# A transformer layer on one core: the loads of its first microseconds queued in another order, later tiles of x loaded into an operand's space, and matrix products of constants put on TensorE

## The chip, the core and the metric

The kernel runs on one core of one Trainium2 chip. Its engines run side by side and meet at semaphores: TensorE (PE in the profile; its weight loads are PEld), VectorE (DVE), ScalarE (ACT), GpSimd (POOL) and SyncE (SP). SP, ACT and POOL also issue DMAs, each from its own queue. SP's and ACT's are hardware queues, POOL's is a software queue.

The metric is the time of one execution on the device in microseconds. A kernel is run several times and the median is taken. Beside these runs one execution is recorded by the hardware profiler, and all rows shown come from that one.

## The reference

One encoder layer over 1024 tokens of width 1024, all in float32: half a step of a gated feed-forward net, a mixture of two kinds of attention, and another half step, each between two RMS norms. What the change touches is the beginning of the first net:

```python
def rmsnorm(x, g):
    xf = x.astype(jnp.float32)
    y = xf * lax.rsqrt(jnp.mean(xf * xf, axis=-1, keepdims=True) + NORM_EPS)
    return (y * g.astype(jnp.float32)).astype(x.dtype)

def swiglu(x, w_gate, w_up, w_down):
    return (jax.nn.silu(x @ w_gate) * (x @ w_up)) @ w_down

h = swiglu(rmsnorm(x, ffn1_pre_g[l]), ffn1_w_gate[l], ffn1_w_up[l], ffn1_w_down[l])
x = x + 0.5 * rmsnorm(h, ffn1_post_g[l])
```

The sum of squares of each token must be known, its root taken, and the token scaled by it and by the gain, before the first product with `w_gate` can be made.

## The kernel before

**Numbers.** A float32 matrix is split into a high part that TensorE takes at its quick type (`float32r`) and a low part, the rest: ScalarE copies the high part, VectorE subtracts it to get the low one. A product is then three: high by high, high by low, low by high. The big products use a seven-product scheme over 2 by 2 blocks, so operands appear as blocks with names: `A11`, `A12`, `A22` are parts of x itself, `S1` to `S4` are sums of parts. `Operand` (line 186) holds them; `self.x[b]` has two tiles, high and low, of 128 x 4 x 512.

**Tiles of x.** x is eight tiles of 128 tokens by 1024 columns. Tiles 0 to 3 are the upper half of the tokens and give `A11` (their left 512 columns) and `A12` (their right 512). Tiles 4 to 7 give the lower half, `A22` and the sums. TensorE transposes each 128 x 128 piece against an identity (`transposed`, line 169; four pieces make one group, PE L174), ScalarE copies the group out as the high part (`transpose_in`, L181), and VectorE makes the low part (L182).

**The head** is the stretch from line 1618 to 1752 in `layer`. In it the orders of PE, DVE and ACT are written out by hand (`ordered(DVE, ACT)`): each of them runs its instructions in the order of the code. After `order.close()` only PE's order stays by hand, and a scheduler places the work of the other engines. POOL's and SP's are always the scheduler's.

1. SP and ACT each load one half of x's tiles 0 and 1 (line 1643: the left halves by SP, the right ones by ACT). SP also loads the gain, one row of 1024 numbers, into the first partition of a tile `xn[0]` (line 1645). ACT loads tile 2 (line 1654), SP tile 3 (line 1655), and SP the first two weights in halves (lines 1653 and 1657) and the third whole (`w2`, line 1658).
2. `spread_gain` (line 342) lays the gain's row out over all 128 partitions by a product: a column of ones, one partition high, by the row, in two halves of 512 columns (L349). Two copies on ScalarE (L350) bring the halves from PSUM to SBUF; the code calls them `gains[0]()` and `gains[1]()` at places of its choice.
3. ScalarE loads its table for the square root (line 1698). It then squares and sums tile 0, and the left half of tile 1 (`square`, L166); VectorE does the right half of tile 1 (L1671). `rstd_by_sqrt` (line 331) adds the halves (L335, L336), takes the root on ScalarE (L337; `next(root)` stops behind it), and refines the reciprocal on VectorE (L324 to L327; the second `next(root)`).
4. `scaled` multiplies a half of a tile by its root and the gain on VectorE (L1678). `op0.one(t, keeps)` transposes a half of tile t and splits it. Copies that only save the transposed tile (`keep`, L264) are put off in the list `keeps`.
5. `hi0`, `lo0` and so on split the halves of the first three weights (L1689 on ScalarE, L1692 on VectorE). `pg.mm` makes products of one weight: for each `k` of four a high by high (L471) and a high by low (L472), then the four low by high (L477). The first products take only 256 columns (tiles 0 and 1), since tiles 2 and 3 come later.
6. `soon` is set for the third weight alone. `self.c.step()` within `mm` runs what is put off in `c.steps`, here the transposes of the right halves of tiles 2 and 3.

**Behind the head**, `pg.ahead` runs the eleven first weights through the products with `A11` and `A12`, while `F(4, 5)` and `F(6, 7)` norm the tiles 4 to 7 (squares L166, scaling L229) and `U(t)` transposes them and builds the blocks `A22` and `S1` to `S4` (`left_half`, `right_half`; casts L303, low parts L304, sums L315 to L318 and L307). The tiles 4 to 7 are loaded by POOL (line 1630) in two pairs into the buffers that tiles 0 to 3 leave. Weights in this stretch are fetched by SP (L495) when a buffer has been split.

**Places.** `Operand.second(place)` (line 197) sets aside the tiles of `S1` to `S4` and `A22` when the stage begins. They are not filled until `right_half` of tile 4. Until then, one tile of `S3` (`place`) holds the first three saved products (`op0.place[:, b]`, line 1745).

**Matmul banks.** `c.psm` has six PSUM banks under one tag, taken in turn; a bank is taken again when all its readers are done.

Of the kernel before, what the change touches and what calls it, by code (L numbers as in the profile page):

```python
# [10 lines left out]
F32 = mybir.dt.float32  # L11
F32R = mybir.dt.float32r
# [6 lines left out]
SEQ, D, DFF = 1024, 1024, 2816  # L19
P, T = 128, 512  # L20
# [8 lines left out]
A11, S2, S1, S4, A12, S3, A22 = range(7)  # L29
# [73 lines left out]
class Weights:  # L103
# [30 lines left out]
    def next(self):  # L134
        return self.ready.popleft()
# [50 lines left out]
class Operand:  # L186
# [2 lines left out]

    def __init__(self, c, gain, which):  # L190
        self.c, self.gain, self.x, self.parts, self.open = c, gain, {}, {}, 0
        self.half, self.raw, self.tied = {}, {}, False
        for b in (A11, A12):
            self.x[b] = [c.xa.tile([P, 4, T], F32R, tag=f"x{b}{i}", name=f"x{b}{i}") for i in range(2)]
        self.saved = [c.dr.tile([P, 2, T], F32, name=f"xn{which}_{t}") for t in range(4)]

    def second(self, place=False):
        tile = self.c.xb.tile
        for b in (S1, S2, S3, S4, A22):
            self.x[b] = [tile([P, 4, T], F32R, tag=f"x{b}{i}", name=f"x{b}{i}") for i in range(1 if place and b == S3 else 2)]  # L200
            if len(self.x[b]) < 2:
                self.place = tile([P, 4, T], F32, tag=f"x{b}1", name="place")

    def norm(self, ts, xs):

# [21 lines left out]
    def tile(self, t, x, xn, r):  # L227
        c, nc = self.c, self.c.nc
        c.behind(lambda: nc.vector.scalar_tensor_tensor(xn, x, r, self.gain, op0=ALU.mult, op1=ALU.mult),  # L229
                 *((DVE,) if self.tied else ()))  # L230
        self.parts[t] = deque(((A11, xn[:, :T]), (A12, xn[:, T:])))
        if t == 4 or t > 4 and c.xn:
            self.early_half(t)
# [58 lines left out]
    def right_half(self, t, src, cols):  # L292

        c, nc = self.c, self.c.nc
        s, x1 = self.half.pop(t)
        if len(self.x[S3]) < 2:
            self.x[S3].append(c.xb.tile([P, 4, T], F32R, tag=f"x{S3}1", name=f"x{S3}1"))
        add, sub = nc.vector.tensor_add, nc.vector.tensor_sub
        a11, a12, a21, s1, s2, s4 = x1[:, 0], x1[:, 1], *[s[:, i] for i in range(4)]

        def split(b, x):
            hi, lo = [h[:, :, cols] for h in self.x[b]]
            nc.scalar.copy(hi, x)  # L303
            sub(lo, x, hi.bitcast(F32))  # L304

        def end():
            sub(s4, a12, s2)  # L307
            split(S4, s4)
            self.open -= 1
            if t == 4 and not c.xn:  # L310
                self.early_half(6)
        a22 = transposed(c, src)
        if t in (4, 5) and not c.xn:
            self.early_half(2 * t - 3)
        add(s1, a21, a22)  # L315
        split(A22, a22)
# [12 lines left out]


def rstd_by_sqrt(c, ss):

    nc, k = c.nc, ss.shape[1]
    h, y, e = [c.small.tile([P, 4], F32, tag=t, name=t)[:, :k] for t in ("v", "y", "e")]
    nc.vector.tensor_add(h, ss[:, :, 0], ss[:, :, 1])  # L335
    nc.vector.tensor_scalar(h, h, 0.5 / D, 0.5 * EPS, op0=ALU.mult, op1=ALU.add)  # L336
    nc.scalar.activation(e, h, AF.Sqrt, scale=2.0)  # L337
    yield
    yield newton(c, y, e, h)


def spread_gain(c, t, row, one):

    nc = c.nc
    copies = []
    for h in range(2):
        sl = slice(h * T, h * T + T)
        ps = c.psm.tile([P, T], F32, tag="mm", name="gps")
        nc.tensor.matmul(ps, one, row[:, sl], start=True, stop=True)  # L349
        copies.append(lambda sl=sl, ps=ps: nc.scalar.copy(t[:, sl], ps))  # L350
    return t, *copies
# [85 lines left out]
class PairGemm:  # L437
# [27 lines left out]
    def mm(self, ps, w, i, a, go_on=False, cols=slice(0, T), ks=range(4), soon=False):  # L465
        hi, lo = w
        xhi, xlo = self.op.x[a]
        mm, out = self.c.nc.tensor.matmul, ps[:, cols]
        for k in ks:
            sl = slice(k * P, (k + 1) * P)  # L470
            mm(out, hi[:, i, sl], xhi[:, k, cols], start=not go_on and k == 0, stop=False, skip_group_check=go_on)  # L471
            mm(out, hi[:, i, sl], xlo[:, k, cols], start=False, stop=False, skip_group_check=go_on)  # L472
            if k == 1 or k == 3 and soon:
                self.c.step()
        for k in ks:
            sl = slice(k * P, (k + 1) * P)
            mm(out, lo[:, i, sl], xhi[:, k, cols], start=False, stop=k == 3, skip_group_check=go_on)  # L477
        if 3 in ks and not soon:
            self.c.step()
# [180 lines left out]
class GatePairs:  # L660

    ties, late, deep, soon = (), (), 3, True
# [340 lines left out]
class QKPairs:  # L1003

    ties, late, deep, soon = (DVE,), (ACT,), 2, False
# [399 lines left out]
def layer(tc, a, out):  # L1405
    nc = tc.nc
    c = Ctx(tc)
    with ExitStack() as ctx:
# [26 lines left out]
        x0 = [a["x"][t * P:(t + 1) * P, :] for t in range(8)]  # L1435
# [186 lines left out]
        with ExitStack() as order:  # L1622
# [1 line left out]
            c.deep, c.xn = 2, 3  # L1624
            c.xp = pool("xp", 2, prep, side="right")

            def load(ts, queues):
                for t, q in zip(ts, queues):
                    xs[t] = c.xp.tile([P, D], F32, tag="x", name="x", bufs=4)
                    q.dma_start(xs[t], x0[t])  # L1630

            half = [slice(0, T), slice(T, D)]
            first_junk = [c.xp.tile([P, D], F32, tag="s", name="junk", bufs=2)]
            w2 = c.xp.tile([P, D], F32, tag="x1", name="w2", bufs=2)
# [2 lines left out]
            xs = {t: c.xp.tile([P, D], F32, tag="x", name="x", bufs=4) for t in range(4)}  # L1637
            xn += [xs[2], xs[3]]
            op0 = Operand(c, None, 0)
            nc.gpsimd.memset(xn[1][:1, :P], 1.0)  # L1640
            for t in range(2):
                for h, q in enumerate((nc.sync, nc.scalar)):
                    q.dma_start(xs[t][:, half[h]], x0[t][:, half[h]])
                    if (t, h) == (0, 0):
                        nc.sync.dma_start(xn[0][:1], a["ffn1_pre_g"])
            op0.gain, *gains = spread_gain(c, gain, xn[0][:1], xn[1][:1, :P])

            def begin(pg):
                for b in range(2):
                    pg.raw[b] = c.wg.tile([P, 2, T], F32, tag="g", name="graw")  # L1650
                pg.raw[2] = w2.rearrange("p (i x) -> p i x", i=2)
                for b in range(2):
                    nc.sync.dma_start(pg.raw[b][:, 0], pg.srcs[b][0][:, half[0]])
                nc.scalar.dma_start(xs[2], x0[2])
                nc.sync.dma_start(xs[3], x0[3])
                for b in range(2):
                    nc.sync.dma_start(pg.raw[b][:, 1], pg.srcs[b][0][:, half[1]])
                nc.sync.dma_start(w2, pg.srcs[2][0])
                ss = [c.small.tile([P, 2, 2], F32, tag="ss2", name="ss2", bufs=2) for _ in range(2)]

                def junk():
# [37 lines left out]
                square(0)  # L1699
                square(1, 0)  # L1700
                square(1, 1, xn[1][:, half[1]])
                gains[0]()
                root = rstd_by_sqrt(c, ss[0])
                next(root)
                (hi0, lo0), (hi1, lo1), (hi2, lo2) = [parts(b) for b in range(3)]
                hi0(0)
                gains[1]()
                square(2)
                r0 = next(root)
                scaled(r0, 0, 0, 1)  # L1710
                lo0(0)
                keeps = []
                op0.one(0, keeps)
                op0.one(1, keeps)
                hi1(0)
                square(3, 0)
                square(3, 1, junk()[:, half[1]])
# [17 lines left out]
                    keeps.pop(0)()  # L1735
                lo2(0)
                scaled(r0, 1, 0, 1)
                load((4, 5), (nc.gpsimd, nc.gpsimd))
                scaled(r1, 1, 2, 3)
                hi2(1)  # L1740
                for b in range(3):
                    if b:
                        c.steps.extend(lambda t=t: op0.one(t, *([keeps] if t > 1 else [])) for t in (2 * b - 2, 2 * b - 1))
                    pg.mm(acc[b], pg.w[b], 0, A11, cols=slice(256 if b < 2 else 0, 512), soon=b == 2)
                    s1.append(pg.save(b, acc[b], op0.place[:, b]))
                    (lo0, lo1, lo2)[b](1)
                while keeps:
                    keeps.pop(0)()
# [2 lines left out]
                order.enter_context(ordered())  # L1751
                return s1
            F = lambda *ts: lambda: op0.norm(ts, [xs[t] for t in ts])
            L, U = (lambda *ts: lambda: load(ts, [nc.gpsimd] * 2)), (lambda t: lambda: op0.put(t))
            op, fin, hs, prep = ffn(1, op0, prep, gate_pairs(1, op0, a["wg1"], a["wu1"], 11), get1,
                                    {0: [F(4, 5), L(6, 7)], 2: [F(6, 7)], 3: [U(4)], 5: [U(5)], 6: [U(6)], 7: [U(7)]},
                                    down_sums(a["wd1"], ts1), value_sums(a["wv"], tsv),
                                    a["ffn1_post_g"], a["mix_pre_g"], x0, x1, begin,
                                    bias_steps(c, *[a[k] for k in ("na_rel_bias", "t5_rel_bias", "onehot", "lncount", "cmask")]))
# [296 lines left out]
```

## Time and profile before

| what | us |
|---|---|
| median of three runs | 1829.14 |
| the runs | 1827.43, 1829.14, 1833.59 |
| the profiled execution | 1829.11 |
| its span, first to last instruction | 1827.3 |
| TensorE busy in the span | 1808.0 |
| TensorE busy from 0 to 12 us | 4.52 |
| TensorE busy from 30 to 80 us | 50.0 |

A row of the timeline gives the start in us, the busy time in us, the engine, the line of the code, the operation, the tile written and the tiles read, shapes, and the number of merged instructions. In square brackets stands the time that the engine was idle just before, and what ended it. A "q" behind an engine's name is its queue of issues. A row of the view of windows gives the stretch, then for PE, PEld, DVE, ACT and POOL the busy time with the number of instructions, then the granted TensorE clock, the share of the DMA engines that was busy, and GB/s. Matmuls overlap, and the ends of matmuls are modelled, so the distance from start to start is a better measure of their speed than their length.

### The profile page before, as it was taken

Reading aid. Unit: us, or ns where it says so; the run is one execution under the profiler, and the core shown is the slowest. Engines: PE = TensorE matmul, PEld = TensorE weight load, DVE = VectorE, ACT = ScalarE, POOL = GpSimd, SP = SyncE. Lnnn points to the kernel's source line nnn. Section 1 sums busy time; section 2 is a strip of 40 time slices with the busy share of each in tenths; the row PEclk is TensorE's granted clock in tenths of the full one; section 3 lists DMA queues with packets and bytes.
Section 4 is the critical chain, followed back from the end, with each engine's and each line's share of the span. In section 5 each row is a group of like instructions: output and inputs, shape, how many; then the busy total and the mean of one; then the engine's idle time right before and its main releaser. Section 6 shows DMA issues by size and latency. Waiting matters only on the chain. (4 is left out here: it accounts for less than half of the span.)

```text
span 1827.3 us, 25167 instructions
## 1 busy us (share of the span) xinstructions
PE 1808.0 (99%) x8876; PEld 1524.0 (83%) x8876; DVE 1309.0 (72%) x2225; ACT 831.5 (46%) x1495; POOL 350.2 (19%) x583
## 2 busy tenths in 40 slices
PE   8999999999999999999999999999999999999998
PEld 6888888888888888888999998888888888888886
DVE  5888876776466878477676856788887777654557
ACT  6622233334443656134688765564223333354433
POOL 2223321112021123232344100121111111110000
PEclk9999999999999999999999999999999999999999
DMA  7756566557888857868687523594655566596564
GB/s 274 255 185 219 165 231 218 208 208 253 308 304 308 285 204 263 266 226 297 196 264 245 190 99 115 184 314 166 196 175 199 198 222 225 182 350 198 191 229 145
DMA packets 172769, 409.28 MB, mean 224 GB/s; under 512 B 20401, under 2 KB 42321, under 8 KB 170594
## 3 DMA queue, kind: packets, MB, share of 16 engines
q1 hardware_dynamic: 124450, 246.07, 40.9%
q0 software_dynamic: 47184, 159.51, 24.0%
q10 hardware_dynamic: 1008, 2.10, 0.3%
q8 instruction: 70, 1.15, 0.2%
q14 instruction: 57, 0.47, 0.1%
HBM read 280.09 MB, written 132.56 MB: 226 GB/s over the span
## 5 line engine op out<-in xcount | busy, mean ns | idle before, releaser
L471 PE MATMUL mmp<-x,whi 128*128 128x512 f32 (+1 forms) x1464 | 571.4, 390 | 0.7 <-ACT x L181 0.7
L472 PE MATMUL mmp<-x,whi 128*128 128x512 f32 (+1 forms) x1464 | 569.2, 389 | 0.7 <-DVE x L182 0.6
L789 PE MATMUL accp<-pw 128*128 128x512 f32 x1800 | 410.9, 390 | 0.0
L789 PEld LDWEIGHTS accp<-pw 128*128 128x128 f32 x1800 | 337.4, 188 | 69.7
L477 PE MATMUL mmp<-x,wlo 128*128 128x512 f32 (+1 forms) x1464 | 390.7, 389 | 0.0
L472 PEld LDWEIGHTS mmp<-x,whi 128*128 128x128 f32 x1464 | 275.9, 188 | 57.5 <-DVE x L182 1.5
L471 PEld LDWEIGHTS mmp<-x,whi 128*128 128x128 f32 x1464 | 275.9, 188 | 56.8 <-ACT x L181 1.3
L477 PEld LDWEIGHTS mmp<-x,wlo 128*128 128x128 f32 x1464 | 274.6, 188 | 56.7 <-DVE wlo L462 0.2
L757 DVE TENSOR_TENSOR pw<-praw,pw 128x1024 fp32r<-128x1024 f32 (+1 forms) x181 | 200.1, 1145 | 129.2 <-ACT pw L756 128.4
L756 ACT CAST pw<-praw 128x1024 fp32r<-128x1024 f32 (+1 forms) x181 | 168.6, 983 | 207.1 <-PE accp L789 163.5
L461 ACT CAST whi<-wraw 128x1024 fp32r<-128x1024 f32 x126 | 132.7, 1053 | 190.4 <-PE mmp L472 164.5
L462 DVE TENSOR_TENSOR wlo<-wraw,whi 128x1024 fp32r<-128x1024 f32 x126 | 153.3, 1218 | 2.5 <-ACT whi L461 2.5
L699 POOL DMA_DIRECT2D g<-sg x44 | 24.0, 545 | 428.7 <-DVE sg L692 243.0
L651 DVE TENSOR_TENSOR c<-mmp,u 128x512 f32<-128x512 f32 x52 | 36.0, 691 | 72.1 <-PE mmp L477 72.1
L461 ACT CAST whi<-traw 128x512 fp32r<-128x512 f32 x52 | 32.3, 621 | 120.7 <-DVE traw L560 92.7
L487 ACT COPY s<-mmp 128x512 f32<-128x512 f32 x49 | 28.8, 588 | 126.2 <-PE mmp L477 120.7
L559 DVE TENSOR_TENSOR wraw<-wraw 128x1024 f32<-128x1024 f32 x52 | 63.7, 1224 | 16.4 <-DMA wraw<-in_wu_dram 15.7
L789 PE MATMUL accp<-pw,x 128*128 128x512 f32 x312 | 71.8, 390 | 0.0
L1091 DVE CUSTOM_DVE_ANT_0 s<-sp,g 128x256 f32<-128x256 f32 (+1 forms) x128 | 48.1, 413 | 30.2 <-PE sp L1188 24.4
L789 PEld LDWEIGHTS accp<-pw,x 128*128 128x128 f32 x312 | 58.3, 188 | 12.3 <-DVE pw L757 0.3
L638 DVE TENSOR_TENSOR c<-mmp,v 128x512 f32<-128x512 f32 x52 | 35.8, 689 | 34.0 <-PE mmp L477 34.0
L1337 PE MATMUL po<-vs,pt 128*128 128x128 f32 x352 | 49.9, 276 | 0.9 <-DVE pt L1103 0.9
(282 smaller groups left out, 2490.8 us busy)
## 6 DMA issues: line engine op xcount, KB each, us to landing
praw<-g SPq DMA_DIRECT2D x70, 512.0 KB
wraw<-in_wg_dram SPq DMA_DIRECT2D x44, 512.0 KB
wraw<-in_wu_dram SPq DMA_DIRECT2D x44, 512.0 KB
tr<-in_wd_dram SPq DMA_DIRECT2D x44, 512.0 KB
g<-sg POOLq DMA_DIRECT2D x88, 256.0 KB, 5.2
ts<-tr POOLq DMA_DIRECT2D x22, 1024.0 KB, 4.7
praw<-ts SPq DMA_DIRECT2D x88, 256.0 KB
praw<-in_wd_dram SPq DMA_DIRECT2D x66, 256.0 KB
```

What stands on the lines that cost most here:

```text
L461: nc.scalar.copy(hi, raw)
L462: nc.vector.tensor_sub(lo, raw, hi.bitcast(F32))
L471: mm(out, hi[:, i, sl], xhi[:, k, cols], start=not go_on and k == 0, stop=False, skip_group_check=go_on)
L472: mm(out, hi[:, i, sl], xlo[:, k, cols], start=False, stop=False, skip_group_check=go_on)
L477: mm(out, lo[:, i, sl], xhi[:, k, cols], start=False, stop=k == 3, skip_group_check=go_on)
L559: nc.vector.tensor_sub(r[:, 0:2], r[:, 1:3], r[:, 0:2])
L651: c.behind(lambda: nc.vector.tensor_add(c21, d, u2), *((DVE,) if self.sink.soon and b == self.n - 1 else ()))
L756: nc.scalar.copy(hi, raw[:, :m])
L757: nc.vector.tensor_sub(lo, raw[:, :m], hi.bitcast(F32))
L789: c.nc.tensor.matmul(acc[t], a, b, start=not chained and gi == 0 and j == i == 0, stop=end and j + n >= len(ops) and i == len(two) - 1, sk ...
L1091: c.nc.vector.tensor_tensor_reduce(out=s, in0=ps, in1=bias, scale=-1.0, scalar=3e38, op0=ALU.add, op1=ALU.min, accum_out=neg)
L1337: nc.tensor.matmul(po[0][:, u], pt[0][:, j, :], vs[:, k0 + j, :], start=j == 0, stop=j == n - 1)
```

## The change

The change does five things, all in the head but for the last.

1. The gain's row is loaded by ACT, third in its queue, behind its halves of tiles 0 and 1. Tiles 2 and 3 are both loaded by SP, each between two halves of weights.
2. Tiles 4 to 7 are loaded by SP, last of the head's loads, into the two tiles of `S4`, which are set aside but not yet in use. `load` and its two uses by POOL are gone. `S3` and `S4` now get both their tiles as operands when `split` first writes them.
3. The ones become a full 128 x 128, and the gain's row is read as a tile of 128 partitions. So the rest of that tile is zeroed first, one half of the columns by VectorE and one by GpSimd, and the row's load follows these.
4. `turn_over` puts products on TensorE whose result nothing reads: 10 of the ones by the ones before the gain's products, 5 of the identity by itself behind them, 3 after a small product that reads the norm's result `r0`, and 2 behind the first transposes.
5. The copy `gains[0]()` moves behind the root's instruction on ScalarE, and within the third weight's products the put-off steps run at `k` 0 and 2 instead of 1 and 3.

```diff
@@ class Operand, second
+            if place and b in (S3, S4):
+                self.place[b] = [tile([P, 4, T], F32, tag=f"x{b}{i}", name="place") for i in range(2)]
+            else:
+                self.x[b] = [tile([P, 4, T], F32R, tag=f"x{b}{i}", name=f"x{b}{i}") for i in range(2)]
@@ right_half
         def split(b, x):
+            if b not in self.x:
+                self.x[b] = [c.xb.tile([P, 4, T], F32R, tag=f"x{b}{i}", name=f"x{b}{i}") for i in range(2)]
@@
+def turn_over(c, x, n):
+
+    ps = c.psm.tile([P, P], F32, tag="mm", name="idle")
+    for _ in range(n):
+        c.nc.tensor.matmul(ps, x, x, start=True, stop=True)
@@ mm
-            if k == 1 or k == 3 and soon:
+            if k in ((0, 2) if soon else (1,)):
                 self.c.step()
@@ layer
-            nc.gpsimd.memset(xn[1][:1, :P], 1.0)
+            nc.gpsimd.memset(xn[1][:, :P], 1.0)
+            for e, h in zip((nc.vector, nc.gpsimd), half):
+                e.memset(xn[0][:, h], 0.0)
             for t in range(2):
                 for h, q in enumerate((nc.sync, nc.scalar)):
                     q.dma_start(xs[t][:, half[h]], x0[t][:, half[h]])
-                    if (t, h) == (0, 0):
-                        nc.sync.dma_start(xn[0][:1], a["ffn1_pre_g"])
-            op0.gain, *gains = spread_gain(c, gain, xn[0][:1], xn[1][:1, :P])
+            nc.scalar.dma_start(xn[0][:1], a["ffn1_pre_g"])
+            turn_over(c, xn[1][:, :P], 10)
+            op0.gain, *gains = spread_gain(c, gain, xn[0], xn[1][:, :P])
+            turn_over(c, c.ident, 5)
@@ begin
-                for b in range(2):
-                    nc.sync.dma_start(pg.raw[b][:, 0], pg.srcs[b][0][:, half[0]])
-                nc.scalar.dma_start(xs[2], x0[2])
+                nc.sync.dma_start(pg.raw[0][:, 0], pg.srcs[0][0][:, half[0]])
+                nc.sync.dma_start(xs[2], x0[2])
+                nc.sync.dma_start(pg.raw[1][:, 0], pg.srcs[1][0][:, half[0]])
                 nc.sync.dma_start(xs[3], x0[3])
...
                 nc.sync.dma_start(w2, pg.srcs[2][0])
+                for t in range(4, 8):
+                    xs[t] = op0.place[S4][t // 6].rearrange("p (i k) x -> p i (k x)", i=2)[:, t % 2]
+                    nc.sync.dma_start(xs[t], x0[t])
...
-                gains[0]()
                 root = rstd_by_sqrt(c, ss[0])
                 next(root)
+                gains[0]()
...
                 r0 = next(root)
+                nc.tensor.matmul(pg.bank()[:, :2], c.ident, r0[:, :2], start=True, stop=True)
+                turn_over(c, c.ident, 3)
                 scaled(r0, 0, 0, 1)
                 lo0(0)
                 keeps = []
                 op0.one(0, keeps)
                 op0.one(1, keeps)
+                turn_over(c, c.ident, 2)
                 hi1(0)
...
-                load((4, 5), (nc.gpsimd, nc.gpsimd))
...
-                    s1.append(pg.save(b, acc[b], op0.place[:, b]))
+                    s1.append(pg.save(b, acc[b], op0.place[S3][1][:, b]))
...
-                                    {0: [F(4, 5), L(6, 7)], 2: [F(6, 7)], 3: [U(4)], 5: [U(5)], 6: [U(6)], 7: [U(7)]},
+                                    {0: [F(4, 5)], 2: [F(6, 7)], 3: [U(4)], 5: [U(5)], 6: [U(6)], 7: [U(7)]},
```

More of the change, by code (lines that the diff above doesn't have):

```diff
@@ L191, in __init__ @@
         self.c, self.gain, self.x, self.parts, self.open = c, gain, {}, {}, 0
-        self.half, self.raw, self.tied = {}, {}, False
+        self.half, self.raw, self.tied, self.place = {}, {}, False, {}
         for b in (A11, A12):
@@ L199, in second @@
         for b in (S1, S2, S3, S4, A22):
-            self.x[b] = [tile([P, 4, T], F32R, tag=f"x{b}{i}", name=f"x{b}{i}") for i in range(1 if place and b == S3 else 2)]
-            if len(self.x[b]) < 2:
-                self.place = tile([P, 4, T], F32, tag=f"x{b}1", name="place")
+            if place and b in (S3, S4):
+                self.place[b] = [tile([P, 4, T], F32, tag=f"x{b}{i}", name="place") for i in range(2)]
+            else:
+                self.x[b] = [tile([P, 4, T], F32R, tag=f"x{b}{i}", name=f"x{b}{i}") for i in range(2)]
     def norm(self, ts, xs):
@@ L1625, in layer @@
             c.xp = pool("xp", 2, prep, side="right")
[L1627 to L1630, printed above, removed]
             half = [slice(0, T), slice(T, D)]
@@ L1753, in layer @@
             F = lambda *ts: lambda: op0.norm(ts, [xs[t] for t in ts])
-            L, U = (lambda *ts: lambda: load(ts, [nc.gpsimd] * 2)), (lambda t: lambda: op0.put(t))
+            U = lambda t: lambda: op0.put(t)
             op, fin, hs, prep = ffn(1, op0, prep, gate_pairs(1, op0, a["wg1"], a["wu1"], 11), get1,
-                                    {0: [F(4, 5), L(6, 7)], 2: [F(6, 7)], 3: [U(4)], 5: [U(5)], 6: [U(6)], 7: [U(7)]},
+                                    {0: [F(4, 5)], 2: [F(6, 7)], 3: [U(4)], 5: [U(5)], 6: [U(6)], 7: [U(7)]},
                                     down_sums(a["wd1"], ts1), value_sums(a["wv"], tsv),
```

2 lines of the change are left out of this document (removed).

## The prediction

> **What bounds the kernel now.** I read the page first, then who kept TensorE waiting after 20 us, then the first 30 us as a timeline.
>
> ```profile
> PE 1808.0 (99%) x8876; PEld 1524.0 (83%) x8876; DVE 1309.0 (72%) x2225; ACT 831.5 (46%) x1495; POOL 350.2 (19%) x583
> PEclk9999999999999999999999999999999999999999
> ```
>
> The view of waits for PE from 20 us to the end (us in total, times, longest) begins so:
>
> ```profile
> PE po L1337 <- DVE pt L1103: 0.9, 1, 0.9
> ```
>
> PE is busy for 99% of 1827.3 us, and behind the head its longest single wait is 0.9 us. So the head alone can give anything, and what it gives passes to the end if no wait takes its place. These are the head's steps, from the timeline (start, us, engine, line, operation, count, idle before it):
>
> ```profile
> 4.20 3.75 PE L349 MATMUL gps<-xn 1*128 1x512 f32 x4 [4.20 <-DMA xn<-in_ffn_pre_g_dram]
> 4.26 1.06 ACT L166 ACTIVATE junk<-x 128x1024 f32<-128x1024 f32 x1 [0.59 <-DMA x<-in_x_dram]
> ...
> 5.22 0.19 ACT L166 ACTIVATION_READ_ACCUMULATOR junk<-x 128x1 f32 x1
> 5.26 0.69 DVE L1671 CUSTOM_DVE_ANT_0 xn<-x 128x512 f32<-128x512 f32 x1 [5.26 <-DMA x<-in_x_dram]
> ...
> 8.08 0.63 ACT L166 ACTIVATE junk<-x 128x512 f32<-128x512 f32 x1 [2.68 <-DMA x<-in_x_dram]
> ...
> 8.71 0.57 ACT L350 COPY gain<-gps 128x512 f32<-128x512 f32 x1
> 8.84 0.16 DVE L335 TENSOR_TENSOR v<-ss 128x2 f32<-128x2 f32 x1 [2.88 <-ACT junk L166]
> ...
> 9.24 0.20 ACT L337 ACTIVATE e<-v 128x2 f32<-128x2 f32 x1
> ...
> 10.34 1.41 DVE L1678 SCALAR_TENSOR_TENSOR xn<-x,y,gain 128x512 f32<-128x512 f32 x2
> ...
> 11.23 1.94 PE L174 MATMUL trp<-ident,xn 128*128 128x128 f32 x8 [3.29 <-DVE xn L1678]
> ...
> 12.36 0.59 ACT L181 CAST x<-trp 128x512 fp32r<-128x512 f32 x1 [0.88 <-PE trp L174]
> ...
> 13.85 0.58 PE L471 MATMUL mmp<-x,whi 128*128 128x256 f32 x1 [0.68 <-ACT x L181]
> ...
> 16.89 1.42 DVE L1678 SCALAR_TENSOR_TENSOR x<-x,y,gain 128x512 f32<-128x512 f32 x2
> ...
> 17.29 1.06 ACT L264 COPY raw<-trp 128x512 f32<-128x512 f32 x2
> ...
> 20.29 0.29 PE L472 MATMUL mmp<-x,whi 128*128 128x256 f32 x1
> ...
> 21.68 0.39 PE L472 MATMUL mmp<-x,whi 128*128 128x256 f32 x1 [0.34 <-DVE x L182]
> ...
> 23.58 0.60 PE L174 MATMUL trp<-ident,xn 128*128 128x128 f32 x4
> ```
>
> Two things are late. First, the left half of x's tile 1 reaches ScalarE at 8.08, the right half, on the other queue, VectorE at 5.26; everything up to the first scaled tile (10.34) hangs on the left. Second, PE is slow at first. This is one line's view (ns shortest, median, longest):
>
> ```profile
> L174 PE MATMUL trp<-ident,xn x16: 270/346/444, 11.2 to 25.3; 128*128 128x128 f32 x16
> ```
>
> Eight transposes take 1.94 us at 11.23, so they start (1.94-0.44)/7 = 0.214 apart; four take 0.60 at 23.58, (0.60-0.27)/3 = 0.11 apart. The granted clock reads full in both, so I go by spacing. The fast rate comes at about 20.29, 6.4 us after dense work began at 13.85.
>
> **The change part by part.** *Loads.* These are the rows of issues, with the ones-tile's memset:
>
> ```profile
> 0.75 0.89 ACTq L1643 DMA_DIRECT2D x<-in_x_dram  x2
> 0.89 0.20 POOL L1640 MEMSET xn<- 1x128 f32 x1
> ...
> 1.21 0.32 SPq L1645 DMA_DIRECT2D xn<-in_ffn_pre_g_dram  x1
> 1.57 0.36 SPq L1643 DMA_DIRECT2D x<-in_x_dram  x1
> 1.67 0.46 ACTq L1654 DMA_DIRECT2D x<-in_x_dram  x1
> ```
>
> Now tile 1's left half stands behind the gain's row on SP, and beside the 512 KB tile 2 on ACT's queue. The change takes both away: SP carries x0, x1, then weights and x2 in turn; ACT carries x0, x1 and the row. I take the left half at 5.3, by the right half's row (between 5.26 and 8.08). The row now waits for memsets of its tile on DVE and POOL; POOL's took 0.20 for 128 columns, so four times that at most for 512: issue near 2.1, landing 3.0 later (1.21 to 4.20) at 5.1. Behind it in ACT's queue stands the table load, which had 0.6 us to spare before x0; I cost it at nothing, 0.3 at worst. The memsets themselves lie in time that DVE (idle until 5.26) and POOL have to spare. Tiles 4 to 7 (2 MB) follow on SP, and go between 12 and 18 us, where these windows show DMA idle (after PEclk: DMA share, GB/s):
>
> ```profile
> 8.00:12.00 4.00, 0.77 (x4) 0.80 (x5) 2.65 (x9) 3.40 (x8) 0.00 (x0) 1.00 1.03 393
> 12.00:14.00 2.00, 1.32 (x7) 0.92 (x5) 1.22 (x3) 1.38 (x3) 0.00 (x0) 1.00 0.16 66
> 14.00:16.00 2.00, 1.85 (x7) 1.56 (x8) 1.86 (x6) 1.30 (x5) 0.00 (x0) 1.00 0.00 0
> ```
>
> Two MB at 393 GB/s are 5.3 us. The loads before them are the same bytes as now, so the last still lands near 12.5; tile 3, needed at about T+1.6 (T below, 12.3), stands ahead of half of these weights, and the last weights are read at T+4.4, 15 us. SP's next issue is this one, and POOL's queue loses four:
>
> ```profile
> 25.55 10.28 SPq L495 DMA_DIRECT2D graw<-in_wg_dram  x3
> ```
>
> So that part costs nothing.
>
> *Norm.* ScalarE squares the left half from 5.41 (the row at 4.26 ends so) to 6.2; VectorE's sum follows at 6.25 instead of 8.84. From there to scaling are 10.34-8.84 = 1.5 us: 7.75, if the gain is there.
>
> *Products.* A product of f32 is two matmuls (the row at 4.20: four for two), each 3.75/4, say 0.86 for 512 columns and 0.214 for 128. PE starts when the ones stand, 1.09 plus a semaphore, 1.3. Before the first transposes it owes 10 products (20 x 0.214 = 4.28), the gain's two (4 x 0.86 = 3.44), 5 (2.14) and 3 (1.28): 11.14 us slow, until 12.44; each us after the clock rises counts double. With 6.4 us to the rise, as this trace has it: 1.3+6.4 = 7.7, and the end is 7.7+(12.44-7.7)/2 = 10.1. So the products, not the norm, hold the first transposes: 10.1 to 10.7. The one small product on the norm's result isn't counted (0.1 perhaps), and the last two products (4 x 0.11) stand behind tile 1's transposes, beside ScalarE's L181, and cost nothing unless the clock is still slow (0.4). [...]
>
> *ScalarE's order.* The gain's first half is copied behind L337 now: PE has it at 5.58+1.72+0.2 = 7.5, so it is copied by 8.1 (0.57 each) and scaling starts at 8.2. Then come one half of w (a copy of the same size), the second copy from 8.6, tile 2's square 9.1 to 10.3 (with its 0.19 reading). The first L181 thus starts at 10.7, by PE, against 12.36: **-1.66**. If PE never held it up, ScalarE's order alone would give 9.6 (6.85, where L337 ends; three copies 0.5 apart; square and reading 1.15): that is the good end, -2.76.
>
> *The chain from the first L181 (T) to L472 at 21.68.* Before, 9.32 us. The second L181 came 0.85 behind the first, as the slow transposes let it; two copies back to back take 1.06, so 0.53: VectorE, which trails it, gains 0.23. Its scaling of tile 2 starts at T+4.53-0.23 = 4.30, done 5.05; four quick transposes, 5.65; ScalarE is free of the copies of L264 at 5.99-0.23 = 5.76. Tile 3 is scaled at 5.72, transposed at 6.32, copied by L181 at 6.94, and its L182, behind tile 2's, ends near 7.75. PE, waiting there, goes on at T+7.75: **-1.57**. VectorE is what is late next.
>
> *Halves.* The last transposes come two matmuls of 512 earlier, 0.23 each:
>
> ```profile
> 25.87 0.39 PE L471 MATMUL mmp<-x,whi 128*128 128x512 f32 x1
> ...
> 26.10 0.39 PE L472 MATMUL mmp<-x,whi 128*128 128x512 f32 x1
> ...
> 28.32 0.59 ACT L181 CAST x<-trp 128x512 fp32r<-128x512 f32 x1 [0.66 <-PE trp L174]
> 28.94 0.69 DVE L182 TENSOR_TENSOR x<-trp,x 128x512 fp32r<-128x512 f32 x1 [0.34 <-ACT x L181]
> ...
> 29.69 0.50 PE L472 MATMUL mmp<-x,whi 128*128 128x512 f32 x1 [0.22 <-DVE x L182]
> ```
>
> ScalarE and VectorE stood idle before these (0.66, 0.34), so L472 comes **0.45** earlier.
>
> *Places.* Tiles 4 to 7 lie in S4's operand until L229 has read them. The first split into it then comes behind that row:
>
> ```profile
> 53.61 0.69 DVE L304 TENSOR_TENSOR x<-s,x 128x512 fp32r<-128x512 f32 x1
> 54.21 2.47 DVE L229 SCALAR_TENSOR_TENSOR xn<-x,y,gain 128x1024 f32<-128x1024 f32 x2
> ...
> 77.88 0.69 DVE L304 TENSOR_TENSOR x<-s,x 128x512 fp32r<-128x512 f32 x1
> ```
>
> The two swap; VectorE works on meanwhile, and 23 us remain until its last split at 77.88. Nothing. If the swap stopped ScalarE's L303 too, 3.7 us of it would be late; banks of PSUM cover some of that. Its first copy of S4 goes into the half that held tiles 4 and 5, read long before, so I take nothing.
>
> **Sum:** -1.66-1.57-0.45 = -3.68. The profiled execution took 1829.11 us (span 1827.3 and 1.8 around it), 0.03 under the median shown. 1829.11-3.68 = **1825.4**.
>
> **Rivals.** *The half of x1 stays late* (a slow DMA engine, not the row or tile 2, held it): scaling at 10.34 as now, the products are done by then, quick transposes end at 11.75: -0.61-1.57-0.45 = -2.63, **1826.5**. For it: no view says which DMA held the half.
>
> *The products become the bound: slower.* If ones and identity don't raise the clock, PE is through at 12.44, slow transposes (3 x 0.214+0.44) give L181 at 13.5, 1.2 later than now, the chain stays 9.32, and only the 0.45 comes off: +0.7, **1829.9**. It decides on that step from a rise later than about 11 us, where the products' end plus 0.6 passes 12.36. For it: 3.75 us of matmuls at 4.20 left slow transposes at 11.23. Against: 3.3 us of idleness lay between (the row at 11.23), and now PE should hardly rest for one.
>
> *The gain is swallowed behind the head*: VectorE is busy almost without a break from 46 to 78 us (third busy time below), and if it could not move up, PE would stand there: **1829.1**. Against it, the operands' last split ends at 78.6 and the first product out of them only arrives here:
>
> ```profile
> 60.00:70.00 10.00, 10.00 (x52) 8.28 (x51) 9.91 (x15) 7.80 (x15) 2.16 (x4) 1.00 0.73 231
> ```
>
> ```profile
> 88.05 0.69 DVE L607 TENSOR_TENSOR u<-mmp,s 128x512 f32<-128x512 f32 x1
> ```
>
> That product takes some 2.7 us, so PE has over 6 us in hand.
>
> *Transposes stay slow*, 0.214 apart whatever else PE does: each of the two groups ahead of L472 ends some 0.5 later than I have it, **1826.4**. The rows speak against it (0.11 at 23.58 against 0.214 at 11.23), so it has 1 in 100, counted with the rest below. [...]
>
> **How the numbers follow.** Forecast 0.70 (own range 1822.6 to 1827.0: from -4.8 by ScalarE's order, less the 1.7 by which the lowest run lies under the median, to the late half of x1); late half 0.12; products as bound 0.08; swallowed 0.05; the rest, another order of VectorE and ScalarE behind the head, 0.05. For 8 in 10: 1822.6 to 1829.2. A measurement of this kernel can tell some 0.3% from no change, 5.5 us: faster than that (under 1823.6) 0.11, slower 0.04, within it 0.85.
>
> **What would show it.** Left half's square on ScalarE by 5.6; first L335 by 6.5; products from 1.3 without a gap to 5.6; spacing 0.11 at the first transposes; first L181 at 10.7; L472 with tile 3 near 18.4; PE even from there on, 3.7 us ahead at 30 and at the end. Transposes 0.214 apart at 10 us, or PE standing on DVE between 30 and 90, would prove me wrong.

## The result, and the profile after

| | median, us | lowest to highest | runs |
|---|---|---|---|
| before, beside the changed kernel | 1827.85 | 1825.45 to 1833.59 | 7 |
| changed | 1834.61 | 1833.31 to 1836.30 | 7 |
| changed, the profiled execution | 1835.66 (span 1833.9) | | 1 |

The ratio is 1.0038, with a 95% interval of 1.0029 to 1.0048: the change costs 6.8 us where 3.7 us less was forecast. The line of the changed kernel's page that answers to that of before:

```profile
PE 1812.5 (99%) x8918; PEld 1526.4 (83%) x8918; DVE 1311.9 (72%) x2226; ACT 832.7 (45%) x1495; POOL 350.1 (19%) x580
```

Its view of waits for PE from 20 us on (us in total, times, longest) begins so:

```profile
PE trp L174 <- ACT raw L265: 1.1, 1, 1.1
PE mmp L479 <- ACT whi L469: 1.0, 1, 1.0
PE po L1345 <- DVE pt L1111: 1.0, 1, 1.0
PE mmp L479 <- ACT s L495: 0.7, 1, 0.7
```

TensorE has 42 matmuls more than the 8876 of before, the products, and at 39 us it now waits for the high part of a weight (`whi`, L469), a wait that the same view of before doesn't have. The head itself, from the timeline (lines have moved: L357 is the old L349, L336 the old L335, L480 the old L472, L469 the old L461):

```profile
0.92 0.48 DVE L1645 MEMSET xn<- 128x512 f32 x1 [0.92 <-PEq L2057]
...
1.14 3.94 PE L347 MATMUL idle<-xn 128*128 128x128 f32 x20 [1.14 <-POOL xn L1643]
1.36 0.52 POOL L1645 MEMSET xn<- 128x512 f32 x1
...
5.89 0.48 ACTq L1649 DMA_DIRECT2D xn<-in_ffn_pre_g_dram  x1
5.93 0.69 DVE L1680 CUSTOM_DVE_ANT_0 xn<-x 128x512 f32<-128x512 f32 x1 [4.53 <-DMA x<-in_x_dram]
6.41 1.28 ACT L1707 ACT_TABLE_LOAD   x1 [6.41 <-DMA x<-in_x_dram]
...
7.93 1.06 ACT L166 ACTIVATE junk<-x 128x1024 f32<-128x1024 f32 x1
...
9.73 0.16 DVE L336 TENSOR_TENSOR v<-ss 128x2 f32<-128x2 f32 x1 [3.09 <-ACT junk L166]
...
11.05 3.63 PE L357 MATMUL gps<-xn 128*128 128x512 f32 x4 [5.97 <-DVE e L327]
13.13 0.59 ACT L358 COPY gain<-gps 128x512 f32<-128x512 f32 x1 [2.81 <-PE gps L357]
...
16.53 1.04 PE L174 MATMUL trp<-ident,xn 128*128 128x128 f32 x8
17.16 1.07 ACT L181 CAST x<-trp 128x512 fp32r<-128x512 f32 x2 [0.81 <-PE trp L174]
```

The row of the same timeline at which PE takes up tile 3:

```profile
25.14 0.39 PE L480 MATMUL mmp<-x,whi 128*128 128x256 f32 x1 [0.34 <-DVE x L182]
```

The gain's row is what is late. Both memsets end by 1.88, yet ScalarE's queue issues the row at 5.89, and everything behind it on that engine waits too: the table load goes at 6.41, where ScalarE had done its first square from 4.26 before. The row lands at 10.92 (the trace's completion events), and PE starts on it at 11.05, after 5.97 us of standing still. "DVE e L327" in that bracket is only what ended nearest in time; the landing is what the product needed. The first L181 comes at 17.16 instead of 12.36, and PE takes up tile 3 (L480) at 25.14 instead of 21.68.

Why 5.89? In the built program the head's sixteen loads by SP and ACT signal eight completion counters, dealt out in turn, and from the ninth load on each waits until the earlier load on its counter has landed. The trace has their landings on eight counters too. The list of ScalarE's instructions, with the waits (`DMAHW2` is counter 2; `DVE` and `Pool` stand for the two memsets):

```
1 L1648 DMA x<-in_x_dram 128x512 x2
2 L1649 DMA xn<-in_ffn_pre_g_dram 1x1024 [waits DMAHW2_49,DVE_49,Pool_49]
3 L1707 ACT_TABLE_LOAD
```

The row's load is the third load in the code's order for ACT and the fifth of all. But it waits for memsets, so the scheduler placed it eleventh, and counter 2 belonged to the right half of x's tile 1, whose last piece landed at 5.79. The trace agrees: on one and the same counter stand the sixteen pieces of that half, from 5.25 to 5.79, and then the row's events, at 6.47 and 10.92.

The second loss is at 39 us. PE's rows there:

```profile
39.30 0.50 PE L479 MATMUL mmp<-x,whi 128*128 128x512 f32 x1 [1.04 <-ACT whi L469]
...
41.77 1.20 PE L485 MATMUL mmp<-x,wlo 128*128 128x512 f32 x4 [0.35 <-DVE wlo L470]
```

ScalarE in the changed kernel:

```profile
36.39 1.28 ACT L686 ACT_TABLE_LOAD   x1
37.68 0.63 ACT L686 ACTIVATE place<-place 128x512 f32<-128x512 f32 x1
38.22 1.03 ACT L469 CAST whi<-graw 128x1024 fp32r<-128x1024 f32 x1
```

ScalarE in the kernel before:

```profile
33.01 1.05 ACT L461 CAST whi<-graw 128x1024 fp32r<-128x1024 f32 x1
34.09 1.28 ACT L678 ACT_TABLE_LOAD   x1
35.38 0.63 ACT L678 ACTIVATE place<-place 128x512 f32<-128x512 f32 x1
```

The copy of the fourth weight now stands behind the table load and a Silu, which the scheduler, not the code, decided. By matching matmuls one to one, PE runs 3.5 us later than in the profile of before at tile 3, 3.0 behind the third weight (here the halves give their 0.5) and 5.1 behind the fourth.

### The profile page after: what moved, and what is told of

Same layout as the page of the kernel before. It is cut to its first block, busy times and chain, and to the rows that moved or that the text cites. A ratio compares the mean times of both kernels' runs of the same rounds, so it can differ in the third digit from the quotient of the medians.

```text
span 1833.9 us, 25247 instructions
## 1 busy us (share of the span) xinstructions
PE 1812.5 (99%) x8918; PEld 1526.4 (83%) x8918; DVE 1311.9 (72%) x2226; ACT 832.7 (45%) x1495; POOL 350.1 (19%) x580
## 3 DMA queue, kind: packets, MB, share of 16 engines
q8 instruction: 70, 1.15, 0.2%
## 5 line engine op out<-in xcount | busy, mean ns | idle before, releaser
L480 PE MATMUL mmp<-x,whi 128*128 128x512 f32 (+1 forms) x1464 | 568.2, 388 | 0.8 <-DVE x L182 0.8
L480 PEld LDWEIGHTS mmp<-x,whi 128*128 128x128 f32 x1464 | 275.0, 188 | 57.1 <-DVE x L182 1.4
L469 ACT CAST whi<-wraw 128x1024 fp32r<-128x1024 f32 x126 | 132.7, 1053 | 189.0 <-PE mmp L480 163.5
L469 ACT CAST whi<-traw 128x512 fp32r<-128x512 f32 x52 | 32.3, 621 | 122.4 <-DVE traw L568 104.8
```

What stands on the lines that cost most here:

```text
L469: nc.scalar.copy(hi, raw)
```

## The experiments

Theories: **the late row** (a wait on ScalarE's queue) against the zeroing and the 128 rows; **the steps** at 0 and 2 by ScalarE's order; the products, places and loads as helps or losses. Every ratio below is to runs of before on the same chip (medians 1827.2, 1827.9 and 1827.3 in the three groups).

**e1, the row set free.** The changed kernel, but the row's tile isn't zeroed, and the gain's product reads one row, as before:

```diff
-            for e, h in zip((nc.vector, nc.gpsimd), half):
-                e.memset(xn[0][:, h], 0.0)
...
-            op0.gain, *gains = spread_gain(c, gain, xn[0], xn[1][:, :P])
+            op0.gain, *gains = spread_gain(c, gain, xn[0][:1], xn[1][:1, :P])
```

> The changed kernel, but the gain's row goes to a tile that is not zeroed, and is spread by ones one partition high, as before. So its load no longer waits for a memset or for the landing of an earlier load. Theory A (row): the row's late issue (5.89 us) held up ScalarE's queue and the first products. Then the row is issued near 1.7, the table load starts by 2.3, the first square at 4.3, the first cast of a transposed tile (L181) at 10 to 11 us instead of 17.2, and TensorE stands 6 to 7 us ahead of the changed kernel at 30 us; the loss at the fourth weight (1.9 us) stays: about 1826 to 1828 in all against 1834.6. Rival B (products): TensorE's 31 idle products hold the transposes up; then L181 comes at 12.5 us or later although the row is early, and the time stays over 1830.

Measured: 1830.26, ratio 1.0019 (1.0010 to 1.0028). The row is issued at 1.67, and some 4 us of the loss are gone. But the time that theory A gave is missed and rival B's holds: over 1830, with the first L181 at 14.13. In this profile the products ran at the slow rate for long, which I take up with e8b. The wait for the fourth weight stays, as expected (1.0 and 0.8 us).

**e6, before with the steps at 0 and 2 alone.**

```diff
-            if k == 1 or k == 3 and soon:
+            if k in ((0, 2) if soon else (1,)):
```

> The kernel before with one edit: within the third weight's products the put-off steps run at k 0 and 2 instead of 1 and 3. Theory A (order): this alone makes the scheduler put ScalarE's copy of the fourth weight (128x1024) behind the table load and the first Silu, and TensorE waits 1 to 2 us for it near 35 us; the last transposes come 0.45 us earlier: +1.4 us in all, 1829 to 1830 against 1827.9. Rival B (load): the copy is late in the changed kernel because the weight's load is late; then this kernel is 0.4 us faster than before, and shows no wait for that copy.

Measured: 1830.02, ratio 1.0017 (1.0008 to 1.0026): 2.8 us slower by this line alone. Its waits for PE from 30 to 60 us:

```profile
PE mmp L477 <- DVE wlo L462: 2.1, 1, 2.1
PE mmp L471 <- ACT whi L461: 1.0, 1, 1.0
```

Before has neither. ScalarE's built order has the weight's copy behind the table load and the Silu, as in the changed kernel. The order, not the half microsecond, is what this edit moves.

**e8, e1 with the old steps** (the line of e6 turned back).

> As the first of these runs, and the steps within the third weight's products at k 1 and 3 as before. Theory A: both losses are gone, TensorE has no wait for the fourth weight's copy and is about 3.2 us ahead of before from 45 us on: 1824 to 1825.5 against 1827.9. Rival B (products, load): no better than before, 1827.5 or more.

Measured: 1827.49, ratio 1.0000 (0.9991 to 1.0010). Its head in the timeline:

```profile
1.67 0.54 ACTq L1647 DMA_DIRECT2D xn<-in_ffn_pre_g_dram  x1
...
5.71 2.20 PE L357 MATMUL gps<-xn 1*128 1x512 f32 x4
...
9.95 1.04 PE L174 MATMUL trp<-ident,xn 128*128 128x128 f32 x8
10.59 1.07 ACT L181 CAST x<-trp 128x512 fp32r<-128x512 f32 x2 [0.57 <-PE trp L174]
...
18.56 0.39 PE L480 MATMUL mmp<-x,whi 128*128 128x256 f32 x1 [0.34 <-DVE x L182]
```

This is the head of the forecast, nearly to the tenth: first L181 at 10.59 (forecast 10.7), tile 3 at 18.56 (18.4). And yet the kernel is no faster than before, which is rival B's result. So even with row and steps as they were meant, the forecast gain isn't there.

**e10, the changed kernel with the old steps** (row late).

> The changed kernel with only the steps put back to k 1 and 3; the row stays late. Theory A (order): the wait for the fourth weight's copy goes (-1.9), the last transposes come 0.45 later: 1833.2 against 1834.6, and TensorE is 3.5 us behind before from 45 us on. Rival B (load): the wait stays, 1835.

Measured: 1833.43, ratio 1.0035 (1.0021 to 1.0049); no wait for the weight remains. Against e8 that prices the late row at 1833.43 - 1827.49 = 5.9 us, give or take some 3 us by the two intervals. In the profiles PE takes up tile 3 at 25.12 in e10 and at 18.56 in e8, 6.6 us apart. The steps cost 2.8 alone (e6, and e1 against e8), but only about 1 on top of the late row (1834.61 - 1833.43 = 1.2). There PE waits 1.04 and 0.35 for the weight, not 1.0 and 2.1; the intervals are too wide to tell that difference apart.

**e13, the row on GpSimd's queue**, with the old steps; tile zeroed, 128 rows:

```diff
-            nc.scalar.dma_start(xn[0][:1], a["ffn1_pre_g"])
+            nc.gpsimd.dma_start(xn[0][:1], a["ffn1_pre_g"])
```

> The changed kernel with the old steps (e10, 1833.4), but the gain's row is loaded on GpSimd's queue, behind its memsets; the tile is still zeroed whole and the product still has 128 rows. Theory A (the row was late because its load waited on ScalarE's queue for a counter that the right half of x1 held): the row is issued near 2.2 and lands by 6.5, the table load goes at 1.7, the first L181 near 11 (up to 14 with a late rise of the clock), and 1827.5 to 1829. Theory B (the zeroing or the 128 rows cost it): the first L181 stays near 17, 1833.

Measured: 1830.23, ratio 1.0014 (1.0005 to 1.0023): 3.2 of the 5.9 us come back (3.9 if each kernel is set against its own runs of before), with the zeroing and the 128 rows still in place. In its timeline:

```profile
2.19 0.67 POOL L1649 DMA_DIRECT2D xn<-in_ffn_pre_g_dram  x1 [0.23 <-POOL ss L1706]
...
7.72 1.95 PE L357 MATMUL gps<-xn 128*128 128x512 f32 x4 [1.93 <-DVE e L327]
...
12.15 1.07 ACT L181 CAST x<-trp 128x512 fp32r<-128x512 f32 x2 [0.66 <-PE trp L174]
```

The wait on ScalarE's queue is confirmed as the larger part, though the time lies above theory A's 1827.5 to 1829. The 128 rows cost nothing that shows: at the slow rate four matmuls over 128 rows took 3.75 us in e10, and over one row 3.75 before. Of the rest the profile shows the flight: issued at 2.19, behind more loads, the row lands at 7.58, not by 6.5. Issue to landing was 2.9 us before (1.21 to 4.07), 5.4 here, 5.0 in the changed kernel. The first L181 is 1.6 us behind e8's; the medians are 2.7 apart (2.0 against each one's own runs of before), and what the remainder is stays open.

**e9, e8 without the products; e7, before with the products alone; e3, the changed kernel without them.** The edit in each is the four calls of `turn_over` and the small product of `r0`.

> The kernel of e8 (row free, old steps) without any of the products that nothing reads. Theory A (a gamble): in e8's own profile the transposes were quick at 9.95 and L480 with tile 3 came at 18.56; in that of e1, with the same products, the fast rate came only at about 13.4 and the first L181 at 14.13. Without the products the first L181 needs only the norm and slow transposes, 10.0 to 10.6, L480 with tile 3 near 19.2 as in e6's profile, and the time doesn't scatter with the clock: 1827.0 to 1828.0, no slower than e8's 1827.5. Theory B (the products are what holds the head where it is): the chain takes 9.3 instead of 8 and the first transposes 0.9 more, 1829 or more.

> The kernel before with the products alone; its loads, row, places and steps are untouched, and ScalarE and VectorE have the very order of before. Theory A: TensorE's products stand ahead of the gain's row, which now starts near 5.7 instead of 4.2, and hold the first transposes until 9 to 13.5 by the instant at which the clock rises; the result is within 1.5 us of before's 1827.2, on the slow side (1827.5 to 1829). Theory B (the forecast's clause): quick transposes give 1.5 us, 1825.7. The profile's other question: does the left half of x's tile 1 land at 8.08 again, as in the one profile of before, or near 6.07 as in that of e6, whose head is the same code? If near 6, the forecast's 2.6 us was one execution's.

> The changed kernel without any of the products that nothing reads; the row's tile is zeroed and its load late as in it, steps at 0 and 2. Theory A: the row sets everything up to the first copy of the gain near 13.1, with or without products (gps took 3.63 at a granted clock of half behind the products, and would take 3.75 cold): 1833.5 to 1835, the clock perhaps rising later. Theory B (idle products that drop the clock are the main loss): 1831 or less.

Measured: e9 1827.48, ratio 1.0000 (0.9991 to 1.0009), equal to e8 with them. e7 1829.42, ratio 1.0013 (1.0004 to 1.0022): behind the old loads the products do harm, some 1.5 us. e3 1833.66, ratio 1.0037 (1.0023 to 1.0050): in the changed kernel they are worth less than can be told. In e9 tile 3 comes at 18.83, in e8 at 18.56.

**e12, before with the places and the early tiles 4 to 7 on SP; e14, before with only the head's loads queued anew and the gain's copy moved.**

> The kernel before with only the places and the early loads of tiles 4 to 7 by SP (S4's two halves; nothing on GpSimd's queue for them). Theory A: it shifts which of the completion counters each later DMA uses, and with that the landing pattern near 670 us, which has PE wait 0.7 to 2.0 us for ScalarE's copy (L495) near 690 in all four kernels with these loads and in neither of the two without: 1828.0 to 1829 and that wait in the profile. Theory B: it costs nothing, 1827.2, and the wait near 690 is chance or comes with the row and the products. The left half of x1 once more: 8.08 or near 6.

> The kernel before with only the head's loads queued anew (x0 and x1 first on both queues, the row third on ScalarE's, free to go; x2 on SP between the weights) and the gain's copy behind L337: no products, no early tiles, old steps. Theory A: the half of x1 lands at 5.3 to 5.5 in every execution, against 6.07, 6.59, 8.07 and 8.08 in the four profiles with the old loads, mean 7.2; that is worth 1 to 2 us: 1825.5 to 1826.8, the one part of the change that gives anything. Theory B: what the head gains is lost again behind it (e8, e9 and e12 all read as before): 1827.2 to 1828.

Measured: e12 1828.16, ratio 1.0002 (0.9994 to 1.0011), and its wait near 690 is 0.3 us. e7, without the places, has 0.7 there and e9, with them, none, so my theory that the places bring this wait falls. e14 1827.01, ratio 0.9999 (0.9990 to 1.0008): above the 1825.5 to 1826.8 that I had hoped for, and no gain by the interval, which leaves room for one of 1.8 us at most. Its runs lie closest together (1826.7 to 1828.2), but no version beats the kernel before by what can be measured.

**e8b and b2: e8 and the kernel before once more, each for one more profile.**

> The kernel of e8 once more, for one more profile. If the instant at which the clock rises is a draw, the first L181 stands anywhere from 10.6 to 14.1 (10.59 in e8, 14.13 in e1, both with the same products); if it is fixed by the kernel, at 10.6 again. The wait of 2.0 us near 686 is absent or shorter (1830.7 was the slowest of eleven, the median 1827.5).

> The kernel before, unchanged, once more for a profile. If the late left half of x1 was a draw of the DMA engines it lands at any time from 6 to 8.1 and L472 with tile 3 goes at 19.2 to 21.7 with it; if it belongs to the kernel, at 8.08 and 21.68 again.

b2 took 1827.98 us. Its head in the timeline, with not a line changed:

```profile
5.99 0.63 ACT L166 ACTIVATE junk<-x 128x512 f32<-128x512 f32 x1 [0.55 <-DMA x<-in_x_dram]
...
9.14 1.94 PE L174 MATMUL trp<-ident,xn 128*128 128x128 f32 x8 [1.25 <-DVE xn L1678]
...
10.26 0.58 ACT L181 CAST x<-trp 128x512 fp32r<-128x512 f32 x1 [0.18 <-PE trp L174]
...
18.98 0.38 PE L472 MATMUL mmp<-x,whi 128*128 128x256 f32 x1 [0.45 <-DVE x L182]
```

The left half of x1 lands at 5.97, not at 8.06, and the first L181 stands at 10.26, ahead of what the forecast promised for the change. The five profiles with the old loads have that square at 8.08, 6.07 (e6), 8.07 (e7), 6.59 (e12) and 5.99. The completion events of the slow ones tell why: a load lands in sixteen pieces, and in the profile of before fifteen had landed by 5.80 and one at 8.06 (e7: by 5.87, and one at 8.05). So one piece of sixteen was over 2 us late, in two executions of five; in e12 one was 0.8 us late (fifteen by 5.75, one at 6.57). With the new loads e8, e8b, e9 and e14 have the square at 5.52 to 5.56, e1 at 5.32 and e13 at 5.29, and in the changed kernel the whole half had landed by 5.60. What held the piece, one slow DMA engine or the loads queued around it, is not shown.

e8b took 1828.58 us, with the first L181 at 11.71 and tile 3 at 19.69: the same kernel as e8, over 1 us later. Three executions have these loads and products: e1, e8 and e8b. The slowest of them, e1, in its timeline:

```profile
1.14 4.63 PE L347 MATMUL idle<-xn 128*128 128x128 f32 x20 [1.14 <-POOL xn L1643]
...
5.71 3.78 PE L357 MATMUL gps<-xn 1*128 1x512 f32 x4
...
12.00 1.63 PE L347 MATMUL idle<-ident 128*128 128x128 f32 x6
13.42 1.12 PE L174 MATMUL trp<-ident,xn 128*128 128x128 f32 x8
14.13 1.07 ACT L181 CAST x<-trp 128x512 fp32r<-128x512 f32 x2 [2.98 <-PE trp L174]
```

These are slow products one behind the other for 12 us, and the quick rate only at the transposes. In e8 the rate doubled inside the gain's product (2.20 at 5.71), in e8b among the first twenty (3.86 us for them, not 4.63). The trace's list of granted clocks puts the rise at 13.57 us in e1, 6.19 in e8 and 4.04 in e8b. So the same loads and products had the rise at 4.04, 6.19 and 13.57 us, and in e1, where it was late, PE waited for its own products. e8b is late for another reason: its clock fell back to half from 7.4 to 10.9 us (last section), just when PE worked off the products ahead of the transposes. Part of e8b's expectation failed: its wait near 686 is 1.8 us again, after 2.0 in e8. Both profiles of this kernel have it, and I haven't found what brings it: ScalarE stands behind a copy (`vt`) that waits for an earlier store of the same buffer to land (1.67 us before 683.03 in e8), and e9, the same but for the products, has none of it.

## Why the prediction was wrong, point by point

- **Loads: the step that failed.** "Issue near 2.1, landing 3.0 later ... at 5.1", and the table load "at nothing, 0.3 at worst". I counted the memsets as the row's only wait. The load also waited for a completion counter, was issued at 5.89 and landed 5.0 later, and the queue behind it (the table load at 6.41, the first square at 7.93) was late with it. Price 5.9 us (e10 against e8), most of the 6.8. The left half itself came as forecast: ScalarE free, it is squared at 5.52 in e8.
- **The base: the size that was wrong even without that.** The gain was measured from a head that held a straggler, 8.08 at the left half, and I took 1829.11 as typical because it lay 0.03 under a median of three runs. Larger sets have 1827.2 to 1827.9. b2's head, without any change, has tile 3 at 18.98, which leaves 0.4 us to e8's 18.56; the profile I worked from (21.68) left 3.1. Against b2's head the changed kernel is 6.2 us late at tile 3, not 3.5. The rival "half of x1 stays late" came near the cause, one late piece of that load; but I asked what it did to the change, not what it did to before.
- **Norm.** L336 at 9.73, not 6.25, all by ScalarE's queue; with the row free it stands at 6.63 (e8: squares from 4.23).
- **Products.** The spacing of transposes at full rate is right: eight in 1.04 at 16.53, (1.04-0.27)/7 = 0.11 apart, so "transposes stay slow" falls. But 6.4 us to the rise was one execution's number. The rival "products become the bound" happened in e1 (L181 at 14.13), one of three with the row free; 0.08 looks too little for it. That its sign was right for the changed kernel is luck, for there PE stood still and waited for the row.
- **Chain.** From the first L181 to tile 3: 7.98 us after (17.16 to 25.14), 7.97 in e8, forecast 7.75. The mechanism is right. But b2 does it in 8.72 without a change, since its clock was up for tile 2's and 3's transposes (eight in 1.15 at 16.27, against 1.91 at 18.37 in the profile I worked from). So 0.75 of the 1.57 was there to gain.
- **Halves: right locally, wrong in sum.** The 0.5 us is seen behind the third weight. That the scheduler, which places ScalarE's work behind the head, would move a weight's copy behind a table load I didn't consider; +2.8 us alone (e6).
- **Places.** Nothing that can be told, as forecast (e12).
- **The gain swallowed behind the head.** e8's profile has PE 3.0 us ahead of before's profile up to 470 us, but 1.6 us behind it at the end. The places where this goes are one wait near 471 (1.3 us, for ScalarE at L818), the wait at 686, and the half clock behind that (1.6 us). Waits of this size also come and go in one kernel: the longest in the profile of before, 0.9 us at L1337, is 2.3 us in b2. Between the medians there is little to explain: tile 3 comes at 18.56 and 19.69 in e8's two profiles, and at 19.19, 19.10 and 18.98 in e6, e12 and b2 with the old loads.

## What to carry to other kernels

A load that gets a new wait can be late by more than that wait, as here, where the memsets had ended by 1.88 and the row was issued at 5.89: look in the built program at what it waits for (a completion counter can be another load's) and at what stands behind it in its engine's queue. A step of two microseconds that hangs on one landing must be seen in several executions before a gain is counted from it; three runs that spread over 6 us, as here, are a warning, though no run shows that this spread came from the head. When the bound engine's order is moved by half a microsecond, compare the orders of the scheduled engines as well, for they may answer with more (2.8 us in e6).

## What the runs showed of the hardware

**The granted clock moved in steps of 3.4 us; what pulls it down stays open.** The windows of the changed kernel (stretch, then PE, PEld, DVE, ACT and POOL, granted clock, DMA share, GB/s):

```profile
6.00:8.00 2.00, 0.00 (x0) 0.00 (x0) 0.64 (x2) 1.55 (x3) 0.00 (x0) 0.90 0.90 319
8.00:10.00 2.00, 0.00 (x0) 0.00 (x0) 0.24 (x2) 1.69 (x4) 0.00 (x0) 0.50 0.99 392
...
12.00:14.00 2.00, 2.00 (x4) 0.93 (x3) 0.25 (x1) 0.87 (x2) 0.00 (x0) 0.50 1.02 412
14.00:16.00 2.00, 2.00 (x15) 1.56 (x15) 1.78 (x3) 1.52 (x3) 0.00 (x0) 0.89 1.04 414
```

A mean of 0.90 is 0.4 us at half and the rest at full, so the clock fell at 7.6, and by the last row it rose at 14.44: 6.84 us at half. The same sums give 6.84 us in e10 and in e7, and about 3.4 in e8b, in e3 (from 18.96) and for e8's wait at 686, whose windows are these:

```profile
688.00:690.00 2.00, 2.00 (x8) 1.64 (x7) 2.00 (x6) 1.86 (x4) 1.25 (x3) 0.71 0.88 328
690.00:692.00 2.00, 2.00 (x6) 1.51 (x6) 2.00 (x5) 0.34 (x1) 0.00 (x0) 0.50 0.92 215
692.00:694.00 2.00, 2.00 (x10) 1.61 (x9) 1.64 (x3) 1.97 (x4) 0.00 (x0) 0.93 0.94 381
```

Once or twice 3.42 us, then. The trace's list of granted clocks has the changed kernel at full from 4.20 for 3.413 us, then at half for 6.827. What pulls the clock down the runs don't settle: ahead of e8's fall PE had stood 2.04 us (to 687.37), and the 0.41 us between e8b's first twenty products and the gain's were all the rest PE had before its fall, while e6 stood 1.0 and 2.1 us and didn't fall. Nor do the early products decide it: e3 has none and fell, and e13 has them, stood 1.93 us behind them and didn't. Nor did the rise come after one length of work: in e8b it took 2.9 us of products (1.15 to 4.04), in e1 12 us of unbroken ones, and in all that time of e1 the record read 1.00 while the spacing was slow. The trace's list of clocks has its first entry only at the rise, so ahead of it the spacing alone tells the rate.

The products do bring the rise forward: to between 4.0 and 6.4 us in six of seven executions with them (13.57 in e1), against 15.5 to 20.3 in the seven without. It gained nothing here (e9 against e8).

**The row of 4 KB on ScalarE's queue moved as one packet.** Its counter shows only two events in the changed kernel, at 6.47 and at 10.92, where a half tile shows sixteen close together (5.25 to 5.79). In the trace the row is one packet of 4096 bytes, begun at 10.29, 4.4 us after its issue, and 0.16 us long; what the event at 6.47 stands for isn't shown. On GpSimd's queue (e13) the same row shows sixteen events, from 6.47 to 7.58, and was no quicker (5.4 us from issue to landing against 5.0). The DMA engines were busy for 0.97 of the time from 5.90 to 10.30. That the 5 us are the wait behind the other loads is my reading; no run shows what stood ahead of the row.
